# Softmax denominators of an attention stage, turned by VectorE and spread through DRAM instead of by TensorE and SBUF

## The chip, the cores and the metric

The kernel runs on one core of a Trainium2 chip. A core has TensorE (PE, matmuls into PSUM), VectorE (DVE), ScalarE (ACT), GpSimd (POOL) and SyncE (SP). SP computes nothing here: it issues DMA transfers, one after the other in the order of its queue, and an entry that has to wait holds everything behind it. The metric is the device time of one execution in microseconds (us); less is better.

## The reference: what is computed

One encoder layer on an input of 512 positions by 1024 features, float32:

```python
h = rms_norm(x, attn_norm_g)
xr, gate, q, k, v = split(h @ w_in)
y_rnn  = (forward RG-LRU scan + backward RG-LRU scan)(conv(xr)) * gelu(gate)
y_attn = dilated_attention(q, k, v, rel_bias)        # 8 heads of 64
x = x + concat(rms_norm(y_rnn), rms_norm(y_attn)) @ w_out
x = x + square(relu(rms_norm(x) @ w_up)) @ w_down
return rms_norm(x, final_norm_g)
```

In the attention, each query sees three dilated windows of keys. The three partial results are combined by their softmax denominators, which is the same as one softmax over all keys with a bias that counts how many windows hold a key. So for each head and each query there is one denominator z, the sum of the exponentials, and the head's output is (sum of exponentials times v) / z.

## The kernel before

Every float32 product is made of three matmuls of split operands (high times high, high times low, low times high; `mm3`, lines 311 to 314). PE's, DVE's, ACT's and POOL's order is written out by hand. In the loop over attention stages SP's order is written out too (line 1141); behind it, the framework places SP's transfers, and it may place some of them among those of the loop.

The 8 heads are worked in 4 pairs p, the two heads of a pair being e = 0 and 1. Stage i of the loop at line 1142 has four steps u. It computes the scores of pair i (`att_s`, PE) and their exponentials (`att_e`, DVE then ACT), and in the same steps turns the exponentials of pair i - 1 (`att_t`: PE transposes of 128x128 into one PSUM bank `pt`, copied by ACT to a tile `ett`; `att_c`: a remaining strip by VectorE's 32x32 transpose). Matmuls of other work, "fillers" (the projections of the next pair, `pqk`, then the output projection, `pwo`), stand between them, so that PE always has something to do. When ACT takes the exponentials, it sums each row into one column of a small tile `zs[p]` (line 814): 128 positions in a tile's partitions, one column for each of four query tiles `qt` and two heads.

The products with v (`att_av`, PE, tile `pav`) leave features in the partitions and queries along the free dimension: partitions 0 to 63 are the head e = 0, partitions 64 to 127 the head e = 1. To divide them, line 947 multiplies by a tile `zrow[p]` of 128x512, which holds 1/z of the partition's head at each query, so the denominators have to be turned by 90 degrees and repeated over 64 partitions. Before the change this goes as follows.

- `att_z(p)`, step u = 0 of stage p + 1: DVE takes the reciprocal of the 8 columns (line 868) and copies each column 16 times into a tile `z16` of 128x128 (line 870).
- `att_t` of the next step, u = 1: PE transposes `z16` in the free quarter of a `pt` bank (line 840), and ACT copies the result back to `z16` (line 845). Partition 32 * qt + 16 * e + r then holds 1/z of the head e at the queries of the tile qt, 16 times over.
- `att_zd(p)`, also at u = 1: SP issues four transfers inside SBUF, one for each qt, each of 32 partitions of 128 numbers read four times over (line 877).

Pairs are divided at different places: `att_av(0)` stands at stage 2, step 0; `att_av(1)` and `att_av(2)` at stage 4, step 0; `att_av(3)` behind the loop (line 1227). After the division of a pair, ACT squares it (`ysq`, line 594), DVE adds the squares (`y_add`, line 600), and after pair 3 PE turns the sum (`pcs`, line 430) for the RMS norm. In stage 4, `emit_dma` (line 230) issues the first loads of the weights `w_up` into tiles `wraw`, and `load_t` (line 1182) loads into tiles `tw`.

Of the kernel before, what the change touches and what calls it, by code (L numbers as in the profile page):

```python
# [12 lines left out]
FT = mybir.dt.float32  # L13
FR = mybir.dt.float32r
AF = mybir.ActivationFunctionType
OP = mybir.AluOpType

P = 128
S = 512
# [79 lines left out]
def hybrid_kernel(ctx: ExitStack, tc, xw0, xw, xn, w_in, w_v, w_out, w_up, w_dn, gates, vecs, bias, fg, out):  # L99
    nc = tc.nc  # L100
# [3 lines left out]
    work = ctx.enter_context(tc.tile_pool(name="work", bufs=1))  # L104
    dram = ctx.enter_context(tc.tile_pool(name="dram", bufs=1, space=bass.MemoryType.DRAM))
# [3 lines left out]
    act = nc.scalar.activation  # L109
# [3 lines left out]
    def g_(name, dt=FT, shape=(P, S)):  # L113
        return work.tile(list(shape), dt, name=name, tag="g", bufs=NG)

    def small(name, w):
        return work.tile([P, w], FT, name=name, tag="sm%d" % w, bufs=8)

    def ps_(name, tag):
        return psum.tile([P, S], FT, name=name, tag=tag, bufs={"pj": 4, "gs": 2, "et": 2}[tag])  # L120
# [12 lines left out]
    ident = consts.tile([P, P], FT, name="ident")  # L133
# [268 lines left out]
    def fan(t, c, n, w):  # L402
        base = t[:, c:c + 1]
        return bass.AP(tensor=base.tensor, offset=base.offset, ap=[base.ap[0]] + ([[1, n]] if n > 1 else []) + [[0, w]])
# [58 lines left out]
    def load_tw(h, v):  # L463
        t = work.tile([P, 1024], FT, name="tw", tag="tw", bufs=4)[:, :2 * WN + TH + P]
        b = nbd.offset + h * 2 * S
        nc.sync.dma_start(t[:, WN:WN + TH + P], bass.AP(tensor=nbd.tensor, offset=b, ap=[[1, P], [1, TH + P]]))
        k = TH - WN - v
        nc.sync.dma_start(bass.AP(tensor=t.tensor, offset=t.offset, ap=[t.ap[0], [WN + TH + P, 2], [1, WN]]),
                          bass.AP(tensor=nbd.tensor, offset=b + S + k, ap=[[1, P], [P - 1 + v - k, 2], [1, WN]]))
        tws[h, v] = t  # L470
# [8 lines left out]
    halves = (slice(0, 64), slice(64, 128))  # L479
# [300 lines left out]
    et, en, zs = {}, {}, {}  # L780
# [7 lines left out]
    def att_s(p, u):  # L788
        qt = QSEQ[u]
        par, far = QT[qt]  # L790
        c0 = P * qt
        w = {(0, 0): TH + TH - WN, (0, 1): 0, (1, 0): TH - WN, (1, 1): TH}[par, far]
        psq[p] = [ps_("ps", "gs") for _ in range(2)]
        for e in range(2):
            k = k_tile(p, e)[:, w:w + NK]
            for i, n in enumerate(("h", "l")):
                nc.tensor.matmul(psq[p][e][:, :NK], lhsT=sp[p, 0, n, e][:, c0:c0 + P], rhs=k, start=i == 0, stop=i == 1)  # L797

    def att_e(p, u):
        qt = QSEQ[u]  # L800
        par, far = QT[qt]
        v = int(par != far)
        if u == 0:
            en[2 * p], en[2 * p + 1] = {}, {}
            zs[p] = small("zz", 8)
        pss = psq.pop(p)
        c0 = (WN + P) * far
        for e in range(2):
            h = 2 * p + e
            t = g_("e")  # L810
            mn = small("mn", 1)
            x = t[:, :NK] if far else t[:, S - NK:]
            nc.vector.tensor_tensor_reduce(x, pss[e][:, :NK], tws[h, v][:, c0:c0 + NK], 1.0, 3.0e38, OP.add, OP.min, mn)
            act(x, x, AF.Exp, scale=-1.0, bias=mn, accum_out=zs[p][:, 2 * qt + e:2 * qt + e + 1])
            en[h][qt] = t
            if u in (1, 3):
                del tws[h, v]
        if u == 3:
            for e in range(2):
                del sp[p, 0, "h", e], sp[p, 0, "l", e], sp[p, 1, "h", e]  # L820
            del kks[p]


    def blocks(jt):
        par, hj = jt // 2, jt % 2
        own = [(2 * (1 - par) + a, (P * hj if a else TH + P * hj)) for a in range(2)]
        oth = [(2 * par + a, (TH + P * hj if a else P * hj)) for a in range(2)]
        return (own + oth, slice(0, NK)) if hj else (oth + own, slice(S - NK, S))

    z16 = {}  # L830

    def att_t(h, jt):
        pt = ps_("pt", "et")
        bs = list(enumerate(blocks(jt)[0]))
        bs.pop(3 if jt % 2 else 0)
        z = z16[h // 2] if (h % 2, jt) == (0, 1) else None
        for i, (qt, k) in bs:
            nc.tensor.transpose(pt[:, i * P:(i + 1) * P], en[h][qt][:, k:k + P], ident)  # L838
        if z is not None:
            nc.tensor.transpose(pt[:, 3 * P:], z, ident)  # L840
        t = et[h, jt] = g_("ett")
        c = slice(bs[0][0] * P, (bs[2][0] + 1) * P)
        act(t[:, c], pt[:, c], AF.Copy)
        if z is not None:
            act(z, pt[:, 3 * P:], AF.Copy)

    def att_c(h, jt):
        hj = jt % 2
        qt = blocks(jt)[0][3 if hj else 0][0]
        c = slice(NK - 32, NK) if hj else slice(S - NK, S - NK + 32)  # L850
        nc.vector.transpose(et[h, jt][:, c], en[h][qt][:, c])
        if jt == 3:
            del en[h]
# [9 lines left out]

    pav, zrow = {}, {}

    def att_z(p):
        rz = small("rz", 8)
        nc.vector.reciprocal(rz, zs.pop(p))
        z16[p] = g_("z16")[:, :P]
        nc.vector.tensor_copy(z16[p], fan(rz, 0, 8, 16))  # L870

    def att_zd(p):
        zrow[p] = g_("zrow")
        t = z16.pop(p)
        for qt in range(4):
            r = t[32 * qt:32 * qt + 32]
            nc.sync.dma_start(zrow[p][:, qt * P:(qt + 1) * P],
                              bass.AP(tensor=r.tensor, offset=r.offset, ap=[r.ap[0], [0, 4], [1, P]]))

    def att_y(p):  # L880
        y_add(1)
# [50 lines left out]
    def att_av(p, jts):  # L932
        if 0 in jts:
            pav[p] = ps_("pav", "gs" if p else "pj")
        for jt in jts:
            parts = av_parts(jt)
            for i, (ci, co) in enumerate(parts):
                for e in range(2):
                    a = slice(64 * e, 64 * e + 64)
                    h = 2 * p + e  # L940
                    nc.tensor.matmul(pav[p][a, co], lhsT=vs[:, jt, h * DH:(h + 1) * DH], rhs=et[h, jt][:, ci],  # L941
                                     start=jt == 0 and i == 0, stop=jt == 3 and i == len(parts) - 1, skip_group_check=True)
            for e in range(2):
                del et[2 * p + e, jt]
        if 3 in jts:
            y = g_("yp")
            nc.vector.tensor_tensor(y[:, ::-1], pav.pop(p), zrow.pop(p), op=OP.mult)
            yat[p] = y
            if p == 3:
                att_a(p)  # L950
            if p != 2:
                att_q(p)
            if p < 2:
                att_a(p)
# [79 lines left out]
    def add_x():  # L1034
        for fn in more.popleft() if more else ():
            fn()
# [83 lines left out]
    def beside(*key):  # L1120
        for e in plan.pop(key, ()):
            e()
# [18 lines left out]
    with tc.manual_schedule(engines={nc.sync.engine}):  # L1141
        for i in range(5):
            for u in range(4):
                if i < 4:
                    att_s(i, u)
                    if u == 2 and i < 3 or u == 0 and i:
                        for e in range(2):
                            load_tw(2 * (i + u // 2) + e, u // 2)
                if i >= 1:
                    att_t(2 * i - 2, u)  # L1150
                    att_t(2 * i - 1, u)
                if i < 4:
                    att_e(i, u)
                if i >= 1:
                    att_c(2 * i - 2, u)
                    att_c(2 * i - 1, u)
                if u == 0 and i >= 1:
                    att_z(i - 1)
                if u == 0:
                    for p in AVS.get(i, ()):  # L1160
                        att_av(p, range(4))
                beside(i, u, 0)
                fill(FILL.get((i, u), (1, 1, 1, 1))[0])
                beside(i, u, 1)
                fill(FILL.get((i, u), (1, 1, 1, 1))[1])
                if u == 1 and i >= 1:
                    att_zd(i - 1)
                if u == 0:
                    for p in AVS.get(i, ()):
                        if p != 2:  # L1170
                            att_y(p)
                beside(i, u, 2)
                fill(FILL.get((i, u), (1, 1, 1, 1))[2])
                beside(i, u, 3)
                fill(FILL.get((i, u), (1, 1, 1, 1))[3])
                add_x()
                beside(i, u, 4)
# [339 lines left out]
    for half in range(2):  # L1517
# [169 lines left out]
        for j in range(7 * NQ):  # L1687
            _, w, q = seq[j]
# [122 lines left out]
```

## Time and profile before

| | |
|---|---|
| median of 3 runs | 530.17 us (529.52 to 530.48) |
| the profiled execution, its own time | 528.82 us |
| its span in the trace | 527.0 us |
| PE busy | 520.1 us, 99% of the span |
| DVE busy | 433.7 us, 82% |
| ACT busy | 357.1 us, 68% |
| POOL busy | 65.8 us, 12% |

The span is the time from the first to the last instruction in the trace; the execution's own time is 1.8 us longer. The attention loop stands at about 109 to 174 us of the span. Instructions on the timeline have a start and a duration. Matmuls overlap: the next one starts before the last one's duration is over, so what a matmul costs PE is read from start to start. A DMA has two times: how long SP is busy issuing it, and how long after that it lands.

### The profile page before, as it was taken

The page shows a single profiled execution, that of the slowest core. Times are in us where ns is not written, and L with a number is a line of the kernel's source. Part 1 is how long each engine was busy: PE and PEld are TensorE (multiplying, and loading weights), DVE is VectorE, ACT ScalarE, POOL GpSimd, SP SyncE. Part 2 cuts the span into 40 slices and gives each one's busy share as a digit, 9 for nine tenths or more (in the row PEclk, how much of TensorE's full clock was granted, in tenths as well). Part 3 has the DMA queues.
Part 4 walks back from the last instruction along what each step waited for, and adds up shares of the span by engine and source line. Part 5 has one row for each costly group of instructions (what it writes and reads, how often), then busy time and mean ns, then how long its engine had stood idle before and what let it go on. Part 6 is the DMA issues. An engine that isn't in the chain of part 4 may idle for free.

```text
span 527.0 us, 8246 instructions
## 1 busy us (share of the span) xinstructions
PE 520.1 (99%) x3001; PEld 448.8 (85%) x3001; DVE 433.7 (82%) x665; ACT 357.1 (68%) x578; POOL 65.8 (12%) x88
## 2 busy tenths in 40 slices
PE   9999999999999999999999999999999999999995
PEld 8856888887887788899999888888999999888884
DVE  5898788997877888898779987889756987987885
ACT  6578983788856757585577755576467677655664
POOL 0184000000000131001300311001101200131000
PEclk9999999999999999999999999999999999999999
DMA  7646446596696498947495899976978497799704
GB/s 285 213 133 162 151 140 189 149 249 190 134 317 208 136 189 230 340 158 203 115 224 142 219 270 274 311 283 160 279 224 217 107 224 214 160 297 265 174 1 159
DMA packets 42441, 106.64 MB, mean 202 GB/s; under 512 B 4865, under 2 KB 15233, under 8 KB 42401
## 3 DMA queue, kind: packets, MB, share of 16 engines
q1 hardware_dynamic: 34848, 80.14, 45.9%
q0 software_dynamic: 7408, 25.79, 26.4%
q8 instruction: 23, 0.38, 0.3%
q10 hardware_dynamic: 144, 0.20, 0.1%
q14 instruction: 18, 0.14, 0.1%
HBM read 94.54 MB, written 4.23 MB: 187 GB/s over the span
## 4 chain that ended last, share of the span: by engine, by line
PE 98%; DVE 0%; issue 0%; DVEq 0%; ACT 0%; ACTq 0%
PE pu L313 10%; PE pu L312 10%; PE pu L314 10%; PE pd L312 10%; PE pd L314 10%; PE pd L313 10%; PE pqk L312 3%; PE pqk L314 3%; PE pqk L313 3%; PE pwo L312 3%; PE pwo L314 3%; PE pwo L313 3%; PE ps L797 2%; PE pav L941 2%; PE pt L838 2%; PE pv L312 2%
## 5 line engine op out<-in xcount | busy, mean ns | idle before, releaser
L269 DVE TENSOR_TENSOR wlo<-wraw,whi 128x1024 fp32r<-128x1024 f32 x71 | 86.6, 1220 | 23.8 <-ACT whi L247 23.5
L247 ACT ACTIVATE whi<-wraw 128x1024 fp32r<-128x1024 f32 x67 | 70.9, 1059 | 32.1 <-PE pd L314 20.2
L313 PE MATMUL pd<-wlo,ah 128*128 128x512 f32 (+1 forms) x195 | 75.2, 386 | 0.0
L312 PE MATMUL pd<-whi,ah 128*128 128x512 f32 (+1 forms) x195 | 75.2, 386 | 0.0
L314 PE MATMUL pd<-whi,al 128*128 128x512 f32 (+1 forms) x195 | 75.2, 386 | 0.0
L247 ACT ACTIVATE whi<-tw 128x1024 fp32r<-128x1024 f32 x38 | 40.2, 1060 | 40.5 <-DMA tw<-in_w_up_dram 12.2
L313 PE MATMUL pu<-hl,whi 128*128 128x256 f32 x224 | 63.4, 283 | 0.0
L314 PE MATMUL pu<-hh,wlo 128*128 128x256 f32 x224 | 63.4, 283 | 0.0
L312 PE MATMUL pu<-hh,whi 128*128 128x256 f32 x224 | 63.4, 283 | 0.0
L269 DVE TENSOR_TENSOR wlo<-tw,whi 128x1024 fp32r<-128x1024 f32 x38 | 46.4, 1220 | 18.6 <-ACT whi L247 18.6
L312 PE MATMUL pu<-h2h,whi 128*128 128x256 f32 (+1 forms) x200 | 60.1, 300 | 0.0
L314 PE MATMUL pu<-h2h,wlo 128*128 128x256 f32 (+1 forms) x200 | 60.0, 300 | 0.0
L313 PE MATMUL pu<-h2l,whi 128*128 128x256 f32 (+1 forms) x200 | 60.0, 300 | 0.0
L312 PEld LDWEIGHTS pu<-hh,whi 128*128 128x128 f32 x224 | 43.0, 192 | 0.0
L313 PEld LDWEIGHTS pu<-hl,whi 128*128 128x128 f32 x224 | 43.0, 192 | 0.0
L314 PEld LDWEIGHTS pu<-hh,wlo 128*128 128x128 f32 x224 | 43.0, 192 | 0.0
L314 PEld LDWEIGHTS pd<-whi,al 128*128 128x128 f32 x195 | 36.6, 188 | 7.4
L313 PEld LDWEIGHTS pd<-wlo,ah 128*128 128x128 f32 x195 | 36.6, 188 | 7.4
L312 PEld LDWEIGHTS pd<-whi,ah 128*128 128x128 f32 x195 | 36.6, 188 | 7.2
L247 ACT ACTIVATE whi<-ts 128x1024 fp32r<-128x1024 f32 x24 | 25.5, 1061 | 24.4 <-PE pd L314 18.1
L312 PEld LDWEIGHTS pu<-h2h,whi 128*128 128x128 f32 x200 | 38.3, 191 | 1.3
L314 PEld LDWEIGHTS pu<-h2h,wlo 128*128 128x128 f32 x200 | 38.3, 191 | 1.3
(276 smaller groups left out, 1246.0 us busy)
## 6 DMA issues: line engine op xcount, KB each, us to landing
wraw<-in_w_up_dram SPq DMA_DIRECT2D x25, 512.0 KB, 4.3
ts<-in_w_dn_dram POOLq DMA_DIRECT2D x24, 512.0 KB, 13.7
wraw<-in_w_dn_dram SPq DMA_DIRECT2D x24, 512.0 KB, 9.1
tw<-in_w_up_dram SPq DMA_DIRECT2D x15, 512.0 KB, 6.7
tw<-in_w_up_dram POOLq DMA_DIRECT2D x15, 512.0 KB, 8.3
wraw<-in_w_in_dram SPq DMA_DIRECT2D x13, 512.0 KB, 3.7
ts<-in_w_dn_dram SPq DMA_DIRECT2D x8, 512.0 KB, 7.1
tw<-in_w_dn_dram SPq DMA_DIRECT2D x8, 512.0 KB, 6.6
```

Source lines behind the costliest of these rows:

```text
L247: act(hi, raws[i], AF.Copy)
L269: nc.vector.tensor_tensor(lo, r, f(splits[i][0]), op=OP.subtract)
L312: nc.tensor.matmul(o, lhsT=a[0], rhs=b[0], start=bool(first), stop=False, skip_group_check=on)
L313: nc.tensor.matmul(o, lhsT=a[0], rhs=b[1], start=False, stop=False, skip_group_check=on)
L314: nc.tensor.matmul(o, lhsT=a[1], rhs=b[0], start=False, stop=bool(last), skip_group_check=on)
L797: nc.tensor.matmul(psq[p][e][:, :NK], lhsT=sp[p, 0, n, e][:, c0:c0 + P], rhs=k, start=i == 0, stop=i == 1)
L838: nc.tensor.transpose(pt[:, i * P:(i + 1) * P], en[h][qt][:, k:k + P], ident)
L941: nc.tensor.matmul(pav[p][a, co], lhsT=vs[:, jt, h * DH:(h + 1) * DH], rhs=et[h, jt][:, ci], start=jt == 0 and i == 0, stop=jt == 3 and i ...
```

## The change

Three of the four moves of the denominators are replaced. The columns of `zs[p]` are ordered by head instead of by query tile. `att_z(p)` takes the reciprocal once, writing each number four times (r = 0 to 3) into a tile of 128x32, with columns in the order e, r, qt. VectorE turns this tile in its four 32x32 squares, and SP writes the result to DRAM (`zd`), where the four copies r of each head become rows of 512 queries: 128 pieces of 32 numbers. `att_zd(p)` issues two transfers, one for each head, that read those four rows 16 times over into the head's 64 partitions. It now stands at u = 2, for the last pair at u = 1 as before. PE's transposes of `z16`, ACT's copies back and the tile `z16` are gone. The new tiles share a tag `zt` of three buffers of their own.

```diff
-            act(x, x, AF.Exp, scale=-1.0, bias=mn, accum_out=zs[p][:, 2 * qt + e:2 * qt + e + 1])
+            act(x, x, AF.Exp, scale=-1.0, bias=mn, accum_out=zs[p][:, 4 * e + qt:4 * e + qt + 1])
...
     def att_t(h, jt):
...
-        z = z16[h // 2] if (h % 2, jt) == (0, 1) else None
...
-        if z is not None:
-            nc.tensor.transpose(pt[:, 3 * P:], z, ident)
...
-        if z is not None:
-            act(z, pt[:, 3 * P:], AF.Copy)
...
+    zd = dram.tile([4, 32, P], FT, name="zd")
+
     def att_z(p):
-        rz = small("rz", 8)
-        nc.vector.reciprocal(rz, zs.pop(p))
-        z16[p] = g_("z16")[:, :P]
-        nc.vector.tensor_copy(z16[p], fan(rz, 0, 8, 16))
+        rz, zt = [work.tile([P, 32], FT, name=n, tag="zt", bufs=3) for n in ("rz", "zt")]
+        z = zs.pop(p)
+        nc.vector.reciprocal(rz.rearrange("p (e r q) -> p e r q", e=2, r=4),
+                             bass.AP(tensor=z.tensor, offset=z.offset, ap=[z.ap[0], [4, 2], [0, 4], [1, 4]]))
+        nc.vector.transpose(zt, rz)
+        nc.sync.dma_start(bass.AP(tensor=zd.tensor, offset=zd.offset + 32 * P * p, ap=[[32, 4], [P, 32], [1, 32]]), zt)
 
     def att_zd(p):
         zrow[p] = g_("zrow")
-        t = z16.pop(p)
-        for qt in range(4):
-            r = t[32 * qt:32 * qt + 32]
-            nc.sync.dma_start(zrow[p][:, qt * P:(qt + 1) * P],
-                              bass.AP(tensor=r.tensor, offset=r.offset, ap=[r.ap[0], [0, 4], [1, P]]))
+        for e in range(2):
+            nc.sync.dma_start(zrow[p][halves[e]], bass.AP(tensor=zd.tensor, offset=zd.offset + 32 * P * p + 4 * S * e, ap=[[0, 16], [S, 4], [1, S]]))
...
-                if u == 1 and i >= 1:
+                if u == (1 if i == 4 else 2) and i >= 1:
                     att_zd(i - 1)
```

More of the change, by code (lines that the diff above doesn't have):

```diff
@@ L828, in blocks @@
         return (own + oth, slice(0, NK)) if hj else (oth + own, slice(S - NK, S))
-    z16 = {}
     def att_t(h, jt):
```

## The prediction

> **What bounds the kernel now.** I read the page first, then the table of busy time by stage around the edit, then the waits of PE's weight loader there, then the timelines.
>
> ```profile
> span 527.0 us, 8246 instructions
> PE 520.1 (99%) x3001; PEld 448.8 (85%) x3001; DVE 433.7 (82%) x665; ACT 357.1 (68%) x578; POOL 65.8 (12%) x88
> PE   9999999999999999999999999999999999999995
> PE 98%; DVE 0%; issue 0%; DVEq 0%; ACT 0%; ACTq 0%
> ```
>
> ```profile
> 100.00:185.00 85.00, 85.00 (x481) 68.88 (x480) 71.66 (x177) 64.69 (x147) 3.40 (x4) 1.00 0.68 197
> ```
>
> The columns of the second fence are the window, the sum, and PE, PEld, DVE, ACT and POOL busy, then the granted clock, DMA share and GB/s. PE is busy in all 85 us around the edit, at a clock of 1.00, and the chain that ended last is PE for 98%. So an edit moves the end in two ways only: it takes work off PE, or it makes PE wait. How much PE's weight loader waits from 100 to 200 us now (total, times, longest, in us):
>
> ```profile
> PEld pav L941 <- issue: 2.4, 12, 0.2
> PEld pwo L312 <- issue: 1.6, 3, 0.7
> PEld pav L941 <- DVE ett L851: 0.4, 1, 0.4
> ```
>
> None of these waits is for a denominator. DVE, ACT, SP and the DMA engines can gain or lose some tenths here without the end seeing it, as long as no operand of PE comes late.
>
> **The change part by part: PE.** Four transposes leave, one for each pair. The same step with and without one:
>
> ```profile
> 114.01 0.49 PE L838 MATMUL pt<-ident,e 128*128 128x128 f32 x3
> 114.34 0.27 PE L840 MATMUL pt<-ident,z 128*128 128x128 f32 x1
> 114.45 0.49 PE L838 MATMUL pt<-ident,e 128*128 128x128 f32 x3
> 114.69 0.48 PE L312 MATMUL pqk<-h_hi,whi 128*128 128x512 f32 x1
> 118.28 0.81 PE L838 MATMUL pt<-ident,e 128*128 128x128 f32 x6
> 118.85 0.48 PE L312 MATMUL pqk<-h_hi,whi 128*128 128x512 f32 x1
> ```
>
> Seven transposes take 114.69 - 114.01 = 0.68 us from the first start to the next filler's start, six take 118.85 - 118.28 = 0.57 us. One costs 0.11 us, and its own row says the same (114.34 to 114.45). Four cost 4 x 0.11 = 0.44 us. The listed duration of 0.27 us is not what it costs, since three of them in a row take 0.49 and not 0.81.
>
> [...]
>
> **ACT and DVE.**
>
> ```profile
> L845 ACT ACTIVATE z<-pt x4: 263/270/273, 115.5 to 169.4; 128x128 f32<-128x128 f32 x4
> L868 DVE RECIPROCAL rz<-zz x4: 159/160/162, 111.8 to 164.5; 128x8 f32<-128x8 f32 x4
> L870 DVE COPY z<-rz x4: 227/227/228, 112.0 to 164.7; 128x128 f32<-128x128 f32 x4
> L851 DVE STREAM_TRANSPOSE ett<-e x32: 167/186/208, 111.6 to 173.5; 128x32 f32<-128x32 f32 x32
> ```
>
> ACT loses four copies of 0.27 us. DVE gives up 0.16 + 0.23 = 0.39 us for each pair, and takes on a reciprocal of 32 instead of 8 numbers in a partition (no such row; between 0.16 and the 0.23 of the 128-wide copy, nearer to the former: 0.18) and one 32x32 turn (0.19): 0.37. Both come to nothing, because PE covers both engines; without that cover, ACT would give 1.1 us back and DVE 0.1. The new order of the columns of `zs` changes no instruction's size. `z16` no longer takes a buffer of the 45 shared ones, so later tiles land in other buffers. I price this at nothing: PE's order is otherwise the same in the two built programs, and the waits that differ point at work that the timelines show finished long before. If one of them did bite, it would be the size of the waits above, 0.2 to 0.7 us.
>
> **SP and the transfers.** SP loses 16 issues (`zrow` by quarters) and gains 4 (`zd`) and 8 (`zrow` by heads).
>
> ```profile
> L877 SPq DMA_DIRECT2D zrow<-z x16: 550/598/1107, 117.5 to 171.9; - x16
> DMA to landing us min/median/max: 2.1/2.1/6.6
> wraw<-in_w_up_dram SPq DMA_DIRECT2D x25, 512.0 KB, 4.3
> hsd<-hsum SPq DMA_DIRECT2D x8, 256.0 KB, 4.9
> hs<-hsd SPq DMA_DIRECT2D x8, 256.0 KB, 6.8
> nbd<-bt POOLq DMA_DIRECT2D x1, 32.0 KB, 2.2
> ```
>
> The nearest rows to the write of `zd` (16 KB from SBUF to DRAM) are `nbd<-bt` (2.2 us to landing) and, far above it in size, `hsd<-hsum` (4.9). I take 2.2, the nearer in size. For the read of `zrow` (128 KB for each head, from DRAM) the bounds are the 2.1 of today's `zrow` and the 6.8 of `hs<-hsd`; between them, I take the 4.3 of a weight load, which may stand ahead of it. An issue costs 0.6, at most 1.1. Now each pair's row against the time at which it is needed:
>
> ```profile
> 122.26 0.43 SPq L468 DMA_DIRECT2D tw<-nbd  x1
> 130.46 0.69 DVE L947 TENSOR_TENSOR yp<-pav,zrow 128x512 f32<-128x512 f32 x1 [0.42 <-PE pav L941]
> 159.35 0.43 SPq L230 DMA_DIRECT2D wraw<-in_w_up_dram  x1
> 159.88 0.85 SPq L1182 DMA_DIRECT2D tw<-in_w_up_dram  x2
> 164.65 0.23 DVE L870 COPY z<-rz 128x128 f32<-128x128 f32 x1
> 169.68 2.78 SPq L877 DMA_DIRECT2D zrow<-z  x4
> 177.10 0.69 DVE L947 TENSOR_TENSOR yp<-pav,zrow 128x512 f32<-128x512 f32 x1
> 179.42 0.69 DVE L600 TENSOR_TENSOR ysq<-ysq 128x512 f32<-128x512 f32 x1
> 180.50 0.60 PE L430 MATMUL pcs<-ident,ysq 128*128 128x128 f32 x4
> 194.13 1.05 ACT L247 ACTIVATE whi<-wraw 128x1024 fp32r<-128x1024 f32 x1
> ```
>
> Pair 0: at u = 2 its two reads stand behind the four `tw` pieces, so they are issued from 122.7 to 123.9 and land between 126.0 and 130.7, 128.2 by my value. The division starts at 130.46. At the worst end it is 0.2 us late. Pairs 1 and 2 are divided in stage 4, when PE has reached the `pav` of both; pair 2 is read in stage 3, and both have more room than pair 0.
>
> Pair 3 is the close one. DVE can have turned the tile at 164.65 + 0.2 = 164.9, where the copy now runs. SP has been free since 159.88 + 0.85 = 160.7. Write of `zd`: issued by 165.5, landed at 167.7. The reads wait for that landing on SP, two issues end at 168.9, landed at 173.2. The division starts at 177.10: 3.9 us to spare. At the far end of every bound: 164.9 + 1.1 + 4.9 + 2 x 1.1 + 6.8 = 179.9, which is 2.8 us late. Today's four issues start at 169.68, since they wait for ACT's copy behind PE's transpose, so the new route starts earlier and is longer.
>
> What waits behind `zd` on SP: in the built order the first `wraw` load of `w_up` moves from ahead of this wait to behind it, 159.35 to about 165.5, and would land at about 170. ACT's first read of such a tile in this stretch is at 194.13, so 6 us of delay are covered by 24. The `zd` entries of pairs 0 to 2 stand behind the `tw` pieces of their step and wait for a DVE result that is ready by then; each costs SP one issue.
>
> **Sum.** PE -0.44, all else 0: the span goes from 527.0 to 526.6 and the profiled execution's own time from 528.82 to 528.4. That execution is 1.35 us under the median of the runs shown, so against the median it is 530.17 - 0.44 = 529.7 us, 0.08% less. A measurement of this kernel can tell about 0.2%, 1.06 us, from no change, so this is "the same".
>
> **The rivals.** *Faster: a transpose costs its whole duration.* If the filler behind the group waits for the last transpose to end, four times 0.272 us, 1.09 us, go: 529.1 us, just past the bound. For it speaks the 0.27 of the row; against it, the two groups side by side above. [...]
>
> *Slower: pair 3's row comes late.* Place: the division at 177.10. Behind it stand ACT's square, DVE's sum, which ends at 179.42 + 0.69 = 180.1, and PE's turn at 180.50, in PE's order ahead of the output projection. PE has 0.4 us of slack; later than 177.5, each microsecond is one of the kernel. At the far end, 2.8 us late, PE stalls 2.4 us: 530.17 - 0.44 + 2.4 = 532.1 us. It decides as "slower" from a stall of 1.5 us on, when the row lands after 179.0, that is 14.1 us after the turn. For it speaks that two transfers now follow each other, with a full landing between, and that loads of 512 KB are on the way: `zrow` has taken 6.6 us once. Against it speaks that nearly every term would have to be at its end at once. [...]
>
> *The same for another reason: PE's gain is lost in a wait of 0.2 to 0.7 us elsewhere*, by the turned buffers. That is 529.9 to 530.4, and no other verdict.
>
> **How the numbers follow.** 0.76 for "the same" (the sum, with the last rival), 0.10 for the whole duration, 0.14 for a late row or a price of the DRAM pieces that I do not see. The range 528.9 to 531.2 holds the first two and the lower part of the third.
>
> **What would show it.** In the profile after, six transposes in every step of the loop with about 0.57 us from first to next filler, no wait of PE or its loader for `pcs` or for DVE's `yp`, pair 3's division starting right behind its `pav`, and PE busy in the whole window from 100 to 185. Right if the landing of `zd` is near 2.2 us. Wrong if the division of pair 3 waits for a DMA, if PE's gain is nearer 1.1 us, or if PE shows a wait that is not there now.

## The result and the profile after

The changed kernel takes 527.97 us (median of 7 runs, 527.45 to 528.25). The kernel before, run beside it, takes 529.90 us (median of 7, 528.45 to 530.48). The ratio is 0.9965 with a 95% interval of 0.9954 to 0.9977: the change makes the kernel faster by 0.35%, 1.93 us. The prediction was 529.7 us, "the same"; the time lies below its range. The profiled execution of the changed kernel takes 527.45 us, 1.37 us less than that of before, and its span is 525.7 us.

The page of the changed kernel (engine, busy time, share, instructions; then the chain that ended last):

```profile
span 525.7 us, 8225 instructions
PE 519.0 (99%) x2997; PEld 447.8 (85%) x2997; DVE 433.8 (83%) x665; ACT 356.1 (68%) x574; POOL 65.7 (13%) x88
...
PE 99%; DVE 0%; issue 0%; DVEq 0%; ACT 0%; ACTq 0%
```

PE still bounds the kernel, with four instructions fewer. Now the steps around the edit, first PE's timeline of the changed kernel, a step that had a transpose of 1/z before:

```profile
113.21 0.82 PE L835 MATMUL pt<-ident,e 128*128 128x128 f32 x6
113.78 0.48 PE L312 MATMUL pqk<-h_hi,whi 128*128 128x512 f32 x1
```

Six transposes, 0.57 us from the first start to the filler's, as in the steps that never had a seventh. Then the rows that the prediction forecast for DVE and SP, in the table of groups, of SP's timeline, and of DVE's around the last pair:

```profile
L864 DVE RECIPROCAL rz<-zz x4: 308/309/309, 111.2 to 163.4; 128x32 f32<-128x32 f32 x4
L866 DVE STREAM_TRANSPOSE zt<-rz x4: 211/212/213, 111.6 to 163.8; 128x32 f32<-128x32 f32 x4
```

```profile
164.01 0.57 SPq L867 DMA_DIRECT2D zd<-zt  x1
164.62 0.46 SPq L230 DMA_DIRECT2D wraw<-in_w_up_dram  x1
166.37 1.17 SPq L872 DMA_DIRECT2D zrow<-zd  x2
```

```profile
175.94 0.69 DVE L941 TENSOR_TENSOR yp<-pav,zrow 128x512 f32<-128x512 f32 x1
178.26 0.69 DVE L600 TENSOR_TENSOR ysq<-ysq 128x512 f32<-128x512 f32 x1
```

The division of pair 3 waits for nothing, and PE is busy for all 85.00 us from 100 to 185 us, as before. So everything that the prediction looked at went about as forecast, and the kernel is 1.9 us faster instead of 0.44. What it did not look at is in the experiments.

### The profile page after: what moved, and what is told of

Same layout as the page of the kernel before. It is cut to its first block, busy times and chain, and to the rows that moved or that the text cites. A ratio compares the mean times of both kernels' runs of the same rounds, so it can differ in the third digit from the quotient of the medians.

```text
span 525.7 us, 8225 instructions
## 1 busy us (share of the span) xinstructions
PE 519.0 (99%) x2997; PEld 447.8 (85%) x2997; DVE 433.8 (83%) x665; ACT 356.1 (68%) x574; POOL 65.7 (13%) x88
## 4 chain that ended last, share of the span: by engine, by line
PE 99%; DVE 0%; issue 0%; DVEq 0%; ACT 0%; ACTq 0%
PE pu L314 10%; PE pu L313 10%; PE pu L312 10%; PE pd L313 10%; PE pd L312 10%; PE pd L314 10%; PE pqk L312 3%; PE pqk L314 3%; PE pqk L313 3%; PE pwo L312 3%; PE pwo L314 3%; PE pwo L313 3%; PE ps L797 2%; PE pav L935 2%; PE pt L835 2%; PE pv L312 2%
## 5 line engine op out<-in xcount | busy, mean ns | idle before, releaser
L313 PEld LDWEIGHTS pu<-h2l,whi 128*128 128x128 f32 x200 | 38.3, 191 | 1.3
```

The lines of the kernel that those rows point to most:

```text
L313: nc.tensor.matmul(o, lhsT=a[0], rhs=b[1], start=False, stop=False, skip_group_check=on)
```

## The experiments

**The two kernels again.** Both profiled executions show one execution each, and differ in more than the change. So both kernels ran again as they are, on a second chip, and once each with a delayed start: 17 warm-up products on PE in place of 8, and 30 idle copies on ACT ahead of the first real work, so that PE's clock would have risen before the work begins. Three theories stood against each other: "Start" (beside the four transposes, the gain is only the moment at which the clock rises), "Body" (the new route is worth about 1.9 us inside the attention stage) and "Program" (that moment belongs to the program).

```diff
-    for _ in range(8):
+    for _ in range(17):
         nc.tensor.matmul(pwarm[:, :P], lhsT=one, rhs=one, start=True, stop=True)
...
+    idle = consts.tile([P, P], FT, name="idle")
+    nc.vector.memset(idle, 0.0)
+    for _ in range(30):
+        act(idle, idle, AF.Copy)
```

> The kernel before, unchanged. Three theories. Start: the edit is worth PE's four transposes (0.35 to 0.45 us), and the rest of the 1.9 us is the moment at which PE's clock reaches full speed at the start (6.58 us into the span in the profile before, 4.81 in the profile after), which falls differently in each execution. Body: the new route is worth about 1.9 us inside the attention stage. Program: the clock's moment belongs to the program, late in the old one, early in the new one. Start expects a ratio of 0.998 to 1.002, a spread over the runs of 1 us or more, and a clock that goes up anywhere from 4.2 to 7.6 us into the span. Body expects 0.999 to 1.001. Program expects the clock to go up near 6.6 us again.

> The changed kernel, unchanged, once more. Start expects a ratio nearer 0.999 than 0.9965 (0.997 to 1.001, by chance), and a clock that goes up somewhere from 4.2 to 7.6 us into the span, not 4.8 again. Body expects 0.9965 again, whatever the clock does. Program expects 0.9965 and a clock that goes up near 4.8 us.

> The kernel before with 17 instead of 8 warm-up products ahead of PE's work, and 30 copies of an unused tile on ACT ahead of its first real operation, so that PE's first real matmul starts about 4 to 5 us later than now, when the clock has gone up in any case. Start and Program expect all real matmuls at full speed, a time 2 to 5 us above the kernel before, and a spread over the runs of less than 1 us. Body expects the same shift and no change of the spread.

> The changed kernel with the same longer warm-up and the same delay. To be read against gate_before, run on the same chip. Start and Program expect it 0.3 to 0.5 us faster than gate_before (0.06 to 0.09%). Body expects 1.5 to 2 us (0.3 to 0.4%).

Measured: the kernel before 529.08 us (12 runs, 528.43 to 530.67), the changed one 527.94 (12 runs, 527.49 to 529.35), ratio to the kernel before on that chip 0.9982 (0.9971 to 0.9993). So the gain is there on another chip too, but 1.14 us by these medians, and 0.98 against the 528.92 of all 23 runs of the kernel before beside them, on which the ratio rests. The two intervals share only 0.9971 to 0.9977. In these two profiles the clock reaches full speed 5.40 and 4.02 us into the span, not 6.58 and 4.81 again, so "Program" is out. "Start" is not: its range for the changed kernel, 0.997 to 1.001, holds this ratio, and the 0.9965 of "Body" did not come again. The 4.2 to 7.6 us that "Start" gave for the clock were the author's estimate; 4.02 lies just under them.

The pair with the delayed start took 539.83 us (538.78 to 541.30) and 538.23 (537.40 to 538.55), five runs each. The delay was badly chosen: PE had finished the warm-up long before ACT let the work begin (it waits 5.7 us for ACT's `h_hi`), and its clock fell to half for 3.4 us, by the 0.90 and 0.53 of the first two rows below. Busy time by stretch of the kernel before with this delay (window, sum, PE, PEld, DVE, ACT, POOL, granted clock, DMA share, GB/s):

```profile
10.00:13.00 3.00, 0.24 (x1) 0.25 (x2) 0.26 (x1) 2.81 (x10) 0.00 (x0) 0.90 0.49 187
13.00:16.00 3.00, 3.00 (x8) 2.36 (x9) 3.00 (x8) 3.00 (x7) 0.00 (x0) 0.53 0.30 85
16.00:19.00 3.00, 3.00 (x15) 2.48 (x14) 3.00 (x6) 3.00 (x7) 0.00 (x0) 1.00 0.17 71
```

So the start was not steadied, though the difference (1.6 us) is what "Body" expected here (1.5 to 2), and not the 0.3 to 0.5 of "Start". The two profiles already show its place: from 162 to 167 us, PE loses 1.1 us in the kernel before that it does not lose in the changed one. It is the stall of the next paragraph.

The repeated kernel before was worth more. Its profile shows a stall that its first profile did not have. Busy time from 150 to 160 us, first in the profile of before that the prediction used, then in the repetition:

```profile
150.00:160.00 10.00, 10.00 (x57) 8.67 (x56) 8.84 (x24) 6.48 (x18) 0.00 (x0) 1.00 0.98 307
```

```profile
150.00:160.00 10.00, 9.34 (x52) 7.62 (x51) 8.40 (x23) 6.10 (x16) 0.00 (x0) 1.00 0.90 268
```

PE is busy for 10.00 and 9.34 us of the ten. The waits of the repetition from 140 to 165 us (engine, line, what for: total us, times, longest):

```profile
DVE x L985 <- DMA x<-in_xn_dram: 1.6, 1, 1.6
PEld ps L797 <- DVE mn L813: 1.4, 3, 1.0
PE ps L797 <- DVE mn L813: 0.7, 1, 0.7
DVE e L813 <- DMA tw<-nbd: 0.6, 1, 0.6
```

PE's scores `ps` of pair 3 wait for DVE's `e`, and DVE waits for transfers: pieces of the bias `tw`, and the tile `x` of the residual. Followed start by start (each matmul against the same one of the first profile), PE falls behind by 1.0 us here. In the changed kernel neither of its two profiles has a wait of PE or of its loader for `ps`. On SP the `tw` pieces stand right behind `zrow` of pair 1. That gave the theory "Stall": SP's four issues for `zrow` hold the `tw` pieces and `x` up, and the change ends that. Its rival "Turns" says that only PE's transposes count.

**The parts one by one.** The next eight kernels all have a delayed start that works (the clock rises at 3.7 to 6.8 us of their profiles, and the first product of the layer starts at 7.6): 17 products, as above, but 15 idle copies instead of 30. Their times are to be compared with each other only, since the delay itself costs some 3 us (532.39 for `s_before`, 529.30 for the kernel before on that chip). First both kernels with it, then the old route with only the new place of the issues (`s_move`), and the new route at the old place (`s_stay`):

```diff
 s_move, against the kernel before
-                if u == 1 and i >= 1:
+                if u == (1 if i == 4 else 2) and i >= 1:
                     att_zd(i - 1)
 s_stay, against the changed kernel
-                if u == (1 if i == 4 else 2) and i >= 1:
+                if u == 1 and i >= 1:
                     att_zd(i - 1)
```

> The kernel before with 17 warm-up products and 15 copies of an unused tile on ACT ahead of its first real operation (30 let PE idle so long that its clock went down again). All real matmuls should now run at full speed, so the spread that the clock's start brings should be gone. Time 2 to 5 us above the kernel before. Stall theory: beside PE's four transposes, the edit removes a stall of PE in stage 3, where the scores' matmuls (ps) wait for DVE's e, which waits for tw and x that SP issued late; it comes in some executions of the kernel before (0.98 us in aa_before, none in the first profile). It expects ps to wait 0 to 1.2 us in all, and a spread over the runs of about 1 us. Turns theory: only PE's transposes count, and the spread is under 0.5 us.

> The changed kernel with the same longer warm-up and the same 15 copies. Stall theory: no wait of ps for e, 0.7 to 1.4 us under s_before in the median, and a spread under 0.7 us. Turns theory: 0.3 to 0.5 us under s_before.

> s_before with one part of the change alone: the four zrow issues of a pair stand at step 2 instead of step 1 (pair 3 at step 1 as before). PE's transposes stay. Place theory (the stall comes from zrow standing ahead of the tw pieces): no wait of ps, time 0.4 to 1.0 us under s_before. Count theory (it comes from four zrow issues instead of two, each taking 0.6 us of SP and one of the eight transfers that SP keeps under way): ps waits as in s_before, same time within 0.3 us.

> s_after with zrow back at step 1 for every pair, all else as changed (DVE turns, DRAM, two issues). Place theory: ps waits again, time 0.4 to 1.0 us above s_after. Count theory: no wait, within 0.3 us of s_after.

| kernel | median us | 12 runs |
|---|---|---|
| s_before | 532.39 | 531.89 to 533.57 |
| s_after | 530.60 | 530.51 to 531.10, and one of 534.04 |
| s_move | 531.17 | 531.09 to 532.25 |
| s_stay | 530.63 | 530.50 to 531.07 |

The whole change is 532.39 - 530.60 = 1.79 us. The move alone brings 532.39 - 531.17 = 1.22 of them, with every transpose still on PE and every issue of the old route still on SP. What is left between `s_move` and the changed kernel is 0.57. The new route at the old place has the whole gain as well. So both of the narrower theories missed once: "Place" expected the wait again in `s_stay`, and "Count" expected it in `s_move`.

The 1.22 us are a difference of medians. In the profile of `s_before` PE loses 0.99 us at this stall, and 0.65 in a second wait, near 492 us, of `pd` for DVE's `x1n`; the profile of `s_move` has neither. The second wait is in the profiles of `s_one` and `s_turn` too (0.4 and 0.3 us), which have no stall, so it is not part of it. How much of the 1.22 is the one and how much the other was not separated.

SP's and DVE's timelines show how. First SP of `s_before`, then of `s_move`:

```profile
139.78 2.54 SPq L881 DMA_DIRECT2D zrow<-z  x4
142.37 0.59 SPq L470 DMA_DIRECT2D tw<-nbd  x1
143.00 0.45 SPq L472 DMA_DIRECT2D tw<-nbd  x1
143.50 1.23 SPq L470 DMA_DIRECT2D tw<-nbd  x1
144.77 0.43 SPq L472 DMA_DIRECT2D tw<-nbd  x1
...
145.81 1.71 SPq L1053 DMA_DIRECT2D x<-in_xn_dram  x2
```

```profile
139.74 0.58 SPq L470 DMA_DIRECT2D tw<-nbd  x1
...
141.36 0.43 SPq L472 DMA_DIRECT2D tw<-nbd  x1
141.89 2.54 SPq L881 DMA_DIRECT2D zrow<-z  x4
...
145.17 1.73 SPq L1053 DMA_DIRECT2D x<-in_xn_dram  x2
```

The last `tw` piece is issued at 145.20 in the one and at 141.79 in the other. DVE's timeline, `s_before` and then `s_move`:

```profile
150.92 0.59 DVE L817 CUSTOM_DVE_ANT_0 e<-ps,tw 128x416 f32<-128x416 f32 x1 [1.16 <-DMA tw<-nbd]
152.85 0.75 DVE L989 SCALAR_TENSOR_TENSOR x<-pwo,rcol,x 128x512 f32<-128x512 f32 x1 [0.77 <-DMA x<-in_xn_dram]
```

```profile
149.69 0.58 DVE L817 CUSTOM_DVE_ANT_0 e<-ps,tw 128x416 f32<-128x416 f32 x1
150.76 0.74 DVE L989 SCALAR_TENSOR_TENSOR x<-pwo,rcol,x 128x512 f32<-128x512 f32 x1
```

Without the two waits DVE is 152.85 - 150.76 = 2.09 us earlier. `x` is needed behind `e` on the same engine, so the lateness adds up. For `tw` the issue is the reason, 3.41 us later. For `x` it is so only in part: `zrow` stands ahead of it in `s_move` too, it is issued 145.81 - 145.17 = 0.64 us later in `s_before`, and then takes 7.1 us to landing instead of 5.4, among transfers that were issued late as well; what slows it there was not tried. In `s_before` it reaches PE 160.42 - 152.85 = 7.57 us after the start of `x`, in its timeline:

```profile
160.42 0.46 PE L801 MATMUL ps<-kk,qh 128*128 128x416 f32 x1 [0.72 <-DVE mn L817]
```

`s_move` has no such wait of PE or its loader. DVE still waits for later `tw` pieces in some kernels without the stall (1.2 us once in the changed kernel's first profile, at 154.74), and PE does not see it.

**Which pair, and how many issues.** `s_one` moves only pair 1's `zrow` in the old kernel. `s_four` has the new route at the old place, with each of its reads split in two, so that SP again issues four transfers.

```diff
 s_one, against s_before
-                if u == 1 and i >= 1:
+                if u == (2 if i == 2 else 1) and i >= 1:
 s_four, against s_stay
-            nc.sync.dma_start(zrow[p][halves[e]], ... offset + 4 * S * e, ap=[[0, 16], [S, 4], [1, S]])
+            for n in range(2):
+                nc.sync.dma_start(zrow[p][halves[e], n * TH:(n + 1) * TH],
+                                  ... offset + 4 * S * e + n * TH, ap=[[0, 16], [S, 4], [1, TH]])
```

> s_before with the four zrow issues of pair 1 alone at step 2, those of the other pairs where they were. If the stall of stage 3 comes from SP issuing pair 1's zrow for 2.5 us ahead of the tw pieces that stage 3 needs, no wait of ps and the time of s_move, 531.2 us. If the other pairs matter, between 531.2 and 532.4.

> s_stay (DVE turns, DRAM, zrow at step 1) with each read of zrow split in two halves of the queries, so that a pair has four issues again. Count theory: SP is held 2.4 us ahead of the tw pieces again, and ps waits again: 531.4 to 532.0 us, that is s_before less PE's turns (0.36) and less 0.2 at the end of the program (20 transfers of this route instead of 16 shift the last one by four of the eight semaphores that SP looks at in order, as 12 do). Route theory (it is the old route's SBUF source or ACT's copy that makes the tw pieces late): 530.6 us as s_stay, no wait.

These two and the next two ran on one more chip, where the kernel before takes 529.22 us against 529.30 on the chip of the four above. `s_one` took 531.15 us (531.06 to 531.75), as much as `s_move`: the one move of pair 1 is the whole effect of the place. `s_four` took 531.72 (530.68 to 533.48), 1.1 us more than `s_stay`, and PE waits for `ps` again. So either half as many issues or a later place is enough. SP of `s_four`, its waits from 140 to 165 us, and DVE's timeline:

```profile
139.70 2.46 SPq L877 DMA_DIRECT2D zrow<-zd  x4
...
143.82 1.07 SPq L472 DMA_DIRECT2D tw<-nbd  x1
```

```profile
PEld ps L801 <- DVE mn L817: 0.5, 1, 0.5
```

```profile
150.69 0.59 DVE L817 CUSTOM_DVE_ANT_0 e<-ps,tw 128x416 f32<-128x416 f32 x1 [1.07 <-PE pt L839]
152.62 0.75 DVE L985 SCALAR_TENSOR_TENSOR x<-pwo,rcol,x 128x512 f32<-128x512 f32 x1 [0.63 <-DMA x<-in_xn_dram]
```

It is the same chain again (the view puts the wait of `e` down to a transpose of PE here, not to `tw`), but in this profile it is small: PE loses 0.4 us by it. More of its 532.87 us lies in two later waits, 1.4 us near 425 us, where `pu` waits for DVE's `wlo`, and 0.5 of `pd` near 492. The wait of `pu` is also in the profiles of `s_noturn`, of `aa_before` and of `gate_after`, which has no stall, so both routes have it in some executions. That the stall returns is shown; that it makes the whole 1.1 us of the medians is not.

**The transposes alone.** `s_turn` puts one transpose, of a constant, back into each pair of the changed kernel, with no copy. `s_noturn` takes the transposes and ACT's copies out of the kernel before.

```diff
 s_turn, against s_after
+        if (h % 2, jt) == (0, 1):
+            nc.tensor.transpose(pt[:, 3 * P:], ident, ident)
 s_noturn, against s_before
-        if z is not None:
-            nc.tensor.transpose(pt[:, 3 * P:], z, ident)
...
-        if z is not None:
-            act(z, pt[:, 3 * P:], AF.Copy)
```

> s_after with four transposes of an unused tile put back on PE at the old places, into the free quarter of pt; nothing reads them. Turns cost 0.09 us each by the traces so far: 0.36 us over s_after, 530.9 to 531.0 us. If one cost its whole 0.27 us: 531.7.

> s_before without PE's four transposes of z16 and ACT's four copies back; zrow is read from the unturned tile at the same places, so the division by the denominators is left out in substance. The turns alone: 0.3 to 0.5 us under s_before (531.9 to 532.1), and ps waits in stage 3 as before. If PE's or ACT's part of the turn made the stall, 530.8 to 531.2.

`s_turn` took 530.93 us (530.89 to 531.29), 0.33 over `s_after`: that is the price of four transposes, 0.08 us each, and its profile followed start by start says 0.35. `s_noturn`, in which `zrow` is filled from unturned numbers, took 532.35 (531.79 to 534.52), as much as `s_before`, where 531.9 to 532.1 was expected. By the trace three of the four transposes lie ahead of the stall. DVE's timeline of `s_noturn` and the waits of PE's loader from 140 to 165 us, in `s_noturn` and then in `s_before`:

```profile
151.36 0.59 DVE L817 CUSTOM_DVE_ANT_0 e<-ps,tw 128x416 f32<-128x416 f32 x1 [1.72 <-DMA tw<-nbd]
```

```profile
PEld ps L801 <- DVE mn L817: 1.7, 3, 0.9
PEld ps L801 <- DVE mn L817: 1.1, 1, 1.1
```

DVE's wait is 1.72 us here and 1.16 in `s_before`, the loader's 1.7 and 1.1. By the traces PE is 0.24 us ahead of `s_before` when it reaches the stall and level with it by 415 us. But not all of that follows from the missing work: `e` starts 0.44 us later than in `s_before` (151.36 against 150.92), so the transfer itself came later in this execution. So the work taken off PE brought nothing that these runs show, while the same work costs 0.33 us where the transfer is early; that an early PE merely waits longer fits this, and is argued.

All 14 profiles together bear out the chain. From the start of the `e` ahead of the two waits to the start of `x` (149.16 to 152.85, 3.69 us, in `s_before`) it takes 1.6 to 3.1 us in the nine profiles in which PE doesn't wait for `ps`, the 3.1 being the first profile of before, and 3.6 to 4.3 us in the five in which it does.

## Why the prediction was wrong

The step that failed stands in its part on what bounds the kernel: "None of these waits is for a denominator. DVE, ACT, SP and the DMA engines can gain or lose some tenths here without the end seeing it, as long as no operand of PE comes late." From one execution without a stall it took the path from SP's issues over DVE to PE to be slack. By its own words an edit moves the end by taking work off PE or by making PE wait; a third way, ending a wait that PE has in other executions, it left out. With it went the part on SP and the transfers, which asks of each moved transfer whether it still comes in time, and never what the issues that go away had held up. SP "loses 16 issues" and gains 12, and the prediction priced the difference at nothing. It was the largest term: the place of the issues alone is worth 1.22 of the 1.79 us in the steady kernels, and halving their number, in `s_stay`, leaves the whole gain as well.

The rows stood in the profile of before. SP's timeline, then DVE's:

```profile
137.48 2.54 SPq L877 DMA_DIRECT2D zrow<-z  x4
140.06 0.59 SPq L466 DMA_DIRECT2D tw<-nbd  x1
...
142.74 2.08 SPq L1049 DMA_DIRECT2D x<-in_xn_dram  x2
```

```profile
148.06 0.59 DVE L813 CUSTOM_DVE_ANT_0 e<-ps,tw 128x416 f32<-128x416 f32 x1 [0.60 <-DMA tw<-nbd]
149.94 0.75 DVE L985 SCALAR_TENSOR_TENSOR x<-pwo,rcol,x 128x512 f32<-128x512 f32 x1 [0.71 <-DMA x<-in_xn_dram]
```

DVE waited 0.60 and 0.71 us for two transfers that stand behind `zrow` on SP. In that one execution PE was not reached, so the profile showed no stall and the step was passed. A hint was there, and the prediction named it without use: the profiled execution was 1.35 us under the median of the runs shown, so the usual execution may have had something that this one lacked. Of the four profiles of the old kernel (two as it is, two with a delayed start) the other three have the stall, 1.0 to 1.1 us of it.

Point by point:

- *PE's four transposes, 0.44 us.* Right in kind, a little large. PE's trace, followed start by start, shows 0.35 less in the first pair of profiles and 0.37 in `s_after` against `s_move`; `s_turn` measured 0.33. The row "0.11" holds, but the matmuls behind the first two win back 0.04 of each.
- *DVE.* The reciprocal takes 0.31 us, not 0.18, and the turn 0.21, not 0.19: 0.52 for each pair instead of 0.37. PE covers it, as said.
- *SP and the last pair.* SP held the reads until 166.37, 1.8 us after `zd` was issued (164.01 + 0.57), where 2.2 was taken; its waits there are 0.9 us for the landing of `zd` and 0.6 for PE's `pav`, and the next `wraw`, which stands behind the reads, was issued at 167.65. The reads took 3.5 to 3.8 us for this pair (5.5 in the median of all eight), where 4.3 was taken. They had landed by 166.37 + 1.17 + 3.8 = 171.3, and the division stands at 175.94: 4.6 us to spare, 3.9 predicted. The first `wraw` moved to 164.62, as said, and nothing waited for it.
- *Buffer turns.* Nothing bites. In the changed kernel the loader waits once for another engine (`pwo`, 0.3 us, for DVE's `x`), as it does in the kernel before; PE itself waits nowhere from 100 to 200 us.
- *The end of the program.* No term of the sum. `s_move` and `s_after` differ by 0.57 us, and the transposes are 0.37 of it. The other 0.2 lies behind the last matmul (next section).
- *The rivals.* The faster one gave 529.1 us by a whole 0.27 us for each transpose. `s_turn` refutes it: 0.08. The time went past it, for a reason that none of the rivals had. The slower one (pair 3's row late) had 4.6 us of room. A price of the DRAM pieces, a part of the prediction's 0.14, no run shows: the write of `zd`, in pieces of 128 bytes, landed within the 1.8 us, and no run wrote the same bytes in larger pieces.

The sum by the runs: 1.22 us for the issues, 0.37 for the transposes and 0.2 at the end make 1.79 with the steadied start. The 1.93 of the first chip is near it. The 1.14 of the second is less, perhaps because the stall is not in every execution; how often it is there was not counted. Why one execution of the same program has it and another not isn't settled either. At that place the DMA engines are busy almost all the time (share 0.98 from 150 to 160 us in the first profile of before), and SP's issues are of different lengths from run to run (the third `tw` piece behind `zrow` took 0.47 us in that profile, 1.23 in `s_before` and 1.68 in `s_noturn`), but neither was tried by itself.

The two profiled executions differ by 1.37 us for other reasons than the medians do. Neither has the stall. The difference is 0.35 for the transposes, 0.2 at the end and 0.82 at the start, which is chance.

## What to carry to other kernels

When a change takes issues off a DMA queue or moves them, look at what stood behind them on that queue and who waits for it, on every engine: here a wait on an engine that is not the bound was the first half of a stall of the one that is (in `s_before`, 1.16 and 0.77 us of DVE ahead of 0.72 of PE). Where the profiled execution is clearly faster than the median, the usual run may have a stall that this profile does not show, and the engines that wait just short of the bound tell where to look; here one more profile of the same kernel showed it. Work taken off the bound ahead of a late operand may buy nothing until the operand is early: `s_noturn` took 532.35 us, `s_before` 532.39.

## What the runs showed of the hardware

**When the clock rises is not the same in each execution.** The trace's record of the granted clock reaches full speed 6.58 us into the span in the profile of before and 5.40 in its repetition, 4.81 in that of after and 4.02 in its repetition, and between 3.7 and 6.8 in the `s_` kernels. The page's rows are too coarse for it, but PE's timeline shows the rate. Before, then after (start, time, x3 is three matmuls together):

```profile
4.47 1.62 PE L443 MATMUL pxr<-h_hi,w3h 128*128 128x512 f32 x3
5.89 1.19 PE L443 MATMUL pxr<-h_lo,w3h 128*128 128x512 f32 x3
```

```profile
4.48 1.08 PE L443 MATMUL pxr<-h_hi,w3h 128*128 128x512 f32 x3
5.40 0.85 PE L443 MATMUL pxr<-h_lo,w3h 128*128 128x512 f32 x3
```

The first three products take 5.89 - 4.47 = 1.42 us in the one and 0.92 in the other; over all of the start PE loses 0.82 us between the two. By these numbers the moments lie 3.1 us apart at most (3.7 to 6.8); what sets them was not tried. With 17 warm-up products and the work begun a little later, most runs of a kernel without the stall lie within 0.25 us of each other (`s_move`: 11 of 12 from 531.09 to 531.33), which is what made 0.3 us measurable here.

**The end of the program differs with the number of transfers.** The last matmul starts at 520.60 of 527.0 us before, and at 519.45 of 525.7 after: 6.40 and 6.25 us to the end by these rounded numbers, 6.44 and 6.23 by the trace's events. The last rows of PE:

```profile
520.60 0.28 PE L314 MATMUL pd<-whi,al 128*128 128x256 f32 x1
```

```profile
519.45 0.28 PE L314 MATMUL pd<-whi,al 128*128 128x256 f32 x1
```

In the trace, SP looks at the semaphores of its transfers in the same order in both profiles before the program ends, eight of them, and the transfers take the eight in turn: 243 of them in the profile of before, 239 in that of after. Its waits for the last one, `out_dram` from `tw`, come to 1.9 us in the one and 1.7 in the other. The route of before has 16 transfers, the new one 12 (`s_four`: 20), so the last transfer's semaphore moves by four places. In all profiles with 16 transfers (`s_move`, `s_one` and `s_noturn` among them) the end takes 6.44 to 6.46 us, and in all with 12 or 20 it takes 6.20 to 6.24. That it is the order of these looks is argued from the events; no run changed the number of transfers alone.
